# Attention of a hybrid encoder's first layer: scores, transposes and value products put into a woven order that is written out by hand for three engines

## The chip, the cores and the metric

The kernel runs as one program on one core of a Trainium2 chip. The metric is the time of one execution on the device in microseconds (us), taken over several runs. The core has five engines that work side by side, each through its own queue in order: TensorE (PE, matrix products and transposes; its weight loads are shown apart as PEld), VectorE (DVE), ScalarE (ACT), GpSimd (POOL), and SyncE (SP), which here only starts transfers. PE writes into PSUM, which the kernel uses as eight banks; here only DVE and ACT read them.

## The reference

Two residual layers, each a token mixer and a convolutional FFN, over 512 tokens of width 1024. The mixer of the first layer is windowed attention with 16 query heads, 4 key heads, width 64 of a head, and a sink logit for each head:

```
q, k, v = split(h @ w_qkv);  q = rope(rms_norm(q));  k = rope(rms_norm(k))
# for each block of 128 queries: the keys of the block before, its own and the next one
sc = q @ k.T * 64**-0.5;  sc = where(abs(qpos - kpos) <= 128, sc, -1e30)
m = max(max(sc), sink);  p = exp(sc - m)
o = (p @ v) / (sum(p) + exp(sink - m))
x = x + o @ w_o;  x = x + conv_ffn(rms_norm(x))
```

The second layer has RWKV-7 time mixing instead of attention. The change touches the attention alone.

## The kernel before

**Order of the work.** A planner (the kernel is built with `schedule_with_timeline_sim=True`, L1525) puts each engine's instructions into an order by its own model of their times; a tile takes the next free buffer of its pool, and waits are put in where data or a buffer needs them. Operations on `nc.any` get their engine from the planner. In the attention nothing else binds the order. (The scan of the second layer already holds each engine to the order of its program text, by a chain of order-only dependencies.)

**Up to the attention.** `swa` (L207) makes q, k and v in three groups `g` of 512 columns: group 0 holds all keys and 4 query heads, group 1 holds 8 query heads, group 2 the last 4 query heads and the values `vn`. For every group and each of 4 token tiles, `heads` (L249) calls `normed` (L223): a square on ACT (L227), a reduce and a scale on DVE (L229, L230), a power on POOL (L231), a product on DVE (L232), the gain on POOL (L233), six small rope operations on DVE (L242 to L247); then a rounded copy on ACT (L264), the remainder on POOL (L265 for groups 1 and 2), four transposes on PE (L271) and a copy out of PSUM on `nc.any` (L278). Groups 0 and 1 are done in place. The four calls for group 2 are kept back (`work`, L343) and stand in the program text ahead of head pairs 1 and 2 (`K.hw = (1, 2)`, L1279): token tiles 0 and 1 before pair 1, tiles 2 and 3 before pair 2. Only pairs 6 and 7 use the query heads of group 2.

**The attention.** The loop at L350 runs over 8 head pairs `hp`, inside it over 4 query blocks `n`, inside it over the 2 heads `e` of the pair. The first and the last block see 2 blocks of keys (256 columns of scores), the two in the middle see 3 (384 columns). For one (n, e): two score products in one PSUM bank (L367) and one product for each masked block (L370); the row maximum on DVE (L373), its negative against the sink (L374, one column), exp with the row sum on ACT (L376). Then for one n: 4 or 6 transposes of p into two banks `tp` (L382), their two copies to `pT` on `nc.any` (L384), and 4 or 6 value products (L387) that use half of the array's columns each (`128*64`; the profile shows two records for each of them) and add into the pair's bank `po`. After the 4 blocks: 1/denominator (L391 to L394), spread over 64 columns on ACT (L396), four transposes (L399), a copy on ACT (L401), the product with `po` on DVE (L402), and the split of the result into a rounded part on ACT (L97) and a remainder on DVE (L98). PSUM: 4 banks `sc`, 2 banks `tp`, 2 banks `mm` (`po` and the output transposes).

**After it.** `out_proj` (L144) multiplies by w_o: 8 output tiles of 24 products of 512 columns (L104 to L106), weights two blocks ahead (`ahead`, L75), in the banks `sc`. Seven eighths of a tile need the results of pairs 0 to 6 only.

Of the kernel before, what the change touches and what calls it, by code (L numbers as in the profile page):

```python
# [8 lines left out]
F32 = mybir.dt.float32  # L9
F32R = mybir.dt.float32r  # L10
BF16 = mybir.dt.bfloat16
AF = mybir.ActivationFunctionType
ALU = mybir.AluOpType
AX = mybir.AxisListType
PSUM = bass.MemoryType.PSUM

P = 128
S = 512
# [4 lines left out]
HD = 64  # L23
NB = 4
# [50 lines left out]
def ahead(K, blocks):  # L75

    raws = [load(K, *b[:2]) for b in blocks[:2]]
    nxt = weights(K, *blocks[0], raws[0])
    for i in range(len(blocks)):
        cur = nxt  # L80
        if i + 2 < len(blocks):
            raws.append(load(K, *blocks[i + 2][:2]))
        if i + 1 < len(blocks):
            nxt = weights(K, *blocks[i + 1], raws[i + 1])
        yield cur
# [10 lines left out]
def split(K, hi, lo, src, lo_engine):  # L96
    K.nc.scalar.copy(out=hi, in_=src)  # L97
    lo_engine.tensor_tensor(out=lo, in0=src, in1=hi.bitcast(F32), op=ALU.subtract)  # L98


def mm3(K, ps, lhs, rhs, first, last):

    nc = K.nc
    nc.tensor.matmul(ps, lhsT=lhs[0], rhs=rhs[0], start=first, stop=False)  # L104
    nc.tensor.matmul(ps, lhsT=lhs[0], rhs=rhs[1], start=False, stop=False)  # L105
    nc.tensor.matmul(ps, lhsT=lhs[1], rhs=rhs[0], start=False, stop=last)  # L106
# [37 lines left out]
def out_proj(K, w, oh, ol, on_tile, bank):  # L144

    for ot, (hi, lo) in enumerate(ahead(K, [(w[i], KT * P, K.nc.vector) for i in range(KT)])):
        ps = bank()
        for kt in range(KT):
            sl = slice(kt * P, (kt + 1) * P)
            mm3(K, ps, (hi[:, sl], lo[:, sl]), (oh[kt], ol[kt]), kt == 0, kt == KT - 1)  # L150
        on_tile(ot, ps)
# [55 lines left out]
def swa(K, x_in, xT, w_qkv, w_o, gains, sinks, rope, cst_mask, on_tile):  # L207
    nc = K.nc
    tc = K.tc
    with ExitStack() as es:  # L210
        ap = es.enter_context(tc.tile_pool(name="swa", bufs=1, reuse_waits="tile"))
        aw = es.enter_context(tc.tile_pool(name="swaw", bufs=2, reuse_waits="tile"))
        sm = es.enter_context(tc.tile_pool(name="swas", bufs=4, reuse_waits="tile"))
        pa = es.enter_context(tc.tile_pool(name="swap", bufs=4, space=PSUM, reuse_waits="tile"))
        pt = es.enter_context(tc.tile_pool(name="swapt", bufs=2, space=PSUM, reuse_waits="tile"))

        qT = K.act.tile([P, 2, KT, S], F32R, name="hl1").rearrange("p a k s -> p (a k) s")
        kT = ap.tile([P, NKV, 2, S], F32R, name="kT")
        vn = ap.tile([P, NB, NKV * HD], F32, name="vn")
# [60 lines left out]
        for g in (0, 1, 2):  # L280
# [33 lines left out]
            if g == 0:  # L314
                K.late()
                gk = ap.tile([P, 2 * HD], F32, name="gk")
                nc.sync.dma_start(out=gk, in_=gains)
                nsk = ap.tile([P, NH], F32, name="nsk")
                nc.sync.dma_start(out=nsk, in_=sinks)
                rp = ap.tile([P, NB, 16], F32, name="rp")  # L320
                nc.sync.dma_start(out=rp, in_=rope)
                mk = aw.tile([P, 2, 384], F32, name="p")[:, 0, 0:2 * P]
                nc.sync.dma_start(out=mk, in_=cst_mask)
                mkb = ap.tile([P, 2 * P], BF16, name="mkb")
                nc.vector.tensor_copy(out=mkb, in_=mk)
                idb = ap.tile([P, P], BF16, name="idb")
                nc.vector.tensor_copy(out=idb, in_=K.ident)
                gq = ap.tile([P, 12, HD], F32, name="gq")
                nc.gpsimd.tensor_copy(out=gq[:, 0:4], in_=gk[:, None, HD:].broadcast_to([P, 4, HD]))
                nc.gpsimd.tensor_scalar(out=gq[:, 4:], in0=gk[:, None, 0:HD].broadcast_to([P, 8, HD]), scalar1=HD ** -0.5,  # L330
                                        scalar2=None, op0=ALU.mult)
                nc.vector.tensor_scalar(out=nsk, in0=nsk, scalar1=-1.0, scalar2=None, op0=ALU.mult)
# [3 lines left out]
            for t in range(NB):  # L336
                nat = aw.tile([P, 512], F32, name="nat", bufs=4)
                nc.scalar.activation(out=nat[:, :w], in_=pss[t][:, :w], func=AF.Copy, scale=rst[:, t:t + 1])
                if g == 2:
                    nc.vector.tensor_scalar(out=vn[:, t], in0=pss[t][:, 256:], scalar1=rst[:, t:t + 1], scalar2=None,  # L340
                                            op0=ALU.mult)
                nats.append(nat)
            work = [(heads, (g, t, nats[t], nk, nh)) for t in range(NB)]  # L343
# [3 lines left out]

        ohl = K.act0.tile([P, 2, KT, S], F32R, name="hl0")
        oh, ol = ohl[:, 0], ohl[:, 1]
        for hp in range(8):  # L350
            if hp in K.hw:
                for fn, args in work[2 * K.hw.index(hp):2 * K.hw.index(hp) + 2]:
                    fn(*args)
            kv = hp // 2
            po = K.pmm.tile([P, NB, P], F32, name="mm")
            nm = sm.tile([P, NB, 2], F32, name="nm")
            den = sm.tile([P, NB, 2], F32, name="den")
            for n in range(NB):
                j0 = 1 if n == 0 else 0
                j1 = 2 if n == NB - 1 else 3  # L360
                bl = [j for j in (0, 2) if j0 <= j < j1]
                p = aw.tile([P, 2, 384], F32, name="p")
                for e in range(2):
                    sc = pa.tile([P, S], F32, name="sc")
                    sv = sc[:, j0 * P:j1 * P]
                    for z in range(2):
                        nc.tensor.matmul(sv, lhsT=qT[:, 2 * hp + e, n * P:(n + 1) * P],  # L367
                                         rhs=kT[:, kv, z, (n - 1 + j0) * P:(n - 1 + j1) * P], start=z == 0, stop=False)
                    for j in bl:
                        nc.tensor.matmul(sc[:, j * P:(j + 1) * P], lhsT=idb, rhs=mkb[:, j * HD:j * HD + P],  # L370
                                         start=False, stop=j == bl[-1])
                    m = sm.tile([P, 1], F32, name="m")
                    nc.vector.tensor_reduce(out=m, in_=sv, axis=AX.X, op=ALU.max)  # L373
                    nc.vector.scalar_tensor_tensor(out=nm[:, n, e:e + 1], in0=m, scalar=-1.0, in1=nsk[:, 2 * hp + e:2 * hp + e + 1],  # L374
                                                   op0=ALU.mult, op1=ALU.min)
                    nc.scalar.activation(out=p[:, e, j0 * P:j1 * P], in_=sv, func=AF.Exp, bias=nm[:, n, e:e + 1],  # L376
                                         accum_out=den[:, n, e:e + 1])
                pT = aw.tile([P, 2, 384], F32, name="pT")
                for e in range(2):
                    tp = pt.tile([P, S], F32, name="tp")  # L380
                    for j in range(j0, j1):
                        nc.tensor.transpose(out=tp[:, j * P:(j + 1) * P], in_=p[:, e, j * P:(j + 1) * P],  # L382
                                            identity=K.ident)
                    nc.any.tensor_copy(out=pT[:, e, j0 * P:j1 * P], in_=tp[:, j0 * P:j1 * P])  # L384
                for j in range(j0, j1):
                    for e in range(2):
                        nc.tensor.matmul(po[e * HD:(e + 1) * HD, n], lhsT=vn[:, n - 1 + j, kv * HD:(kv + 1) * HD],  # L387
                                         rhs=pT[:, e, j * P:(j + 1) * P], start=n == 0 and j == j0,
                                         stop=n == NB - 1 and j == j1 - 1)
            es_ = sm.tile([P, NB, 2], F32, name="es")  # L390
            nc.vector.tensor_tensor(out=es_, in0=nm, in1=nsk[:, None, 2 * hp:2 * hp + 2].broadcast_to([P, NB, 2]), op=ALU.subtract)  # L391
            nc.scalar.activation(out=es_, in_=es_, func=AF.Exp)
            nc.vector.tensor_tensor(out=den, in0=den, in1=es_, op=ALU.add)
            nc.vector.reciprocal(out=den, in_=den)  # L394
            o = aw.tile([P, NB, P], F32, name="o")
            nc.scalar.copy(out=o.rearrange("p n (e d) -> p n e d", e=2), in_=den[:, :, :, None].broadcast_to([P, NB, 2, HD]))  # L396
            oT = K.pmm.tile([P, NB, P], F32, name="mm")
            for n in range(NB):
                nc.tensor.transpose(out=oT[:, n], in_=o[:, n], identity=K.ident)  # L399
            o = aw.tile([P, NB, P], F32, name="o").rearrange("p n q -> p (n q)")  # L400
            K.e_o(out=o, in_=oT.rearrange("p n q -> p (n q)"))  # L401
            nc.vector.tensor_tensor(out=o, in0=po.rearrange("p n q -> p (n q)"), in1=o, op=ALU.mult)  # L402
            split(K, oh[:, hp], ol[:, hp], o, nc.vector)
        out_proj(K, w_o, [oh[:, i] for i in range(KT)], [ol[:, i] for i in range(KT)], on_tile,
                 lambda: pa.tile([P, S], F32, name="sc"))

# [1123 lines left out]
```

## Time and profile before

| what | value |
|---|---|
| three timed runs | 1616.32, 1618.85 (median), 1850.56 us |
| profiled execution, its own time | 1614.49 us |
| its span, first to last instruction | 1612.3 us |
| mean granted PE clock | 0.944 |
| busy PE / DVE / ACT / POOL | 92% / 64% / 43% / 27% of the span |
| attention, first scores to last value products | about 82.6 to 192.6 us of the span |

A row of a timeline gives start, duration, engine, line, operation, output<-input and count, with the idle time before it in square brackets where there was any. Durations on one engine overlap: the next instruction of a stream starts before the one ahead of it has ended, so the distance between two starts, not the duration, is what an instruction takes from its engine. A PE that is busy all the time is therefore not PE at its peak.

### The profile page before, as it was taken

What the parts mean: (1) busy time and instruction counts of PE and PEld (TensorE: products, weight loads), DVE (VectorE), ACT (ScalarE), POOL (GpSimd) and SP (SyncE); (2) the same over time, 40 slices, a digit from 0 to 9 for tenths busy, and PEclk for the clock granted to TensorE, in tenths of its full rate; (3) what the DMA queues carried; (4) which work ended last, traced back from release to release, by engine and by line L of the source; (5) the groups of instructions that cost most, each with busy time, mean ns of one, the idle gap of its engine ahead of it and who ended that gap; (6) DMA issues with size and microseconds to landing.
All of it is one profiled execution on the core that took longest, in us unless ns stands there. A gap on an engine that the chain in (4) does not pass through costs nothing. (4 is left out here: it accounts for less than half of the span.)

```text
span 1612.3 us, 28487 instructions
## 1 busy us (share of the span) xinstructions
PE 1479.9 (92%) x11612; PEld 1195.5 (74%) x11612; DVE 1035.2 (64%) x1642; ACT 687.3 (43%) x1227; POOL 442.2 (27%) x533
## 2 busy tenths in 40 slices
PE   8999999999999998989986678888589999999999
PEld 7767688888888886767764577777467788888887
DVE  6876447777763348968988557667256677777222
ACT  5576534444442223655543333434334444444111
POOL 2630002322310015425498422332200323222000
PEclk9999999999999999999986588888899999999999
DMA  5200033223333322446546545555532222333341
GB/s 191 75 27 1 18 92 97 96 92 105 92 98 117 108 83 68 138 157 217 177 143 199 160 107 145 147 142 147 165 106 84 91 92 91 97 99 101 101 121 56
DMA packets 108978, 179.09 MB, mean 111 GB/s; under 512 B 49200, under 2 KB 62128, under 8 KB 108848
## 3 DMA queue, kind: packets, MB, share of 16 engines
q1 hardware_dynamic: 108704, 177.27, 35.6%
q8 instruction: 91, 1.49, 0.4%
q14 instruction: 39, 0.32, 0.1%
q10 hardware_dynamic: 144, 0.00, 0.0%
HBM read 142.91 MB, written 34.34 MB: 110 GB/s over the span
## 5 line engine op out<-in xcount | busy, mean ns | idle before, releaser
L68 ACT CAST whi<-wraw 128x1024 fp32r<-128x1024 f32 (+2 forms) x196 | 200.3, 1023 | 275.5 <-PE mm L105 179.4
L71 DVE TENSOR_TENSOR wlo<-wraw,whi 128x1024 fp32r<-128x1024 f32 (+2 forms) x139 | 167.6, 1207 | 183.4 <-ACT whi L68 182.7
L104 PE MATMUL mm<-hl,whi 128*128 128x512 f32 x720 | 281.3, 391 | 1.5 <-DVE xT L1360 0.9
L106 PE MATMUL mm<-hl,wlo 128*128 128x512 f32 x720 | 281.5, 391 | 0.5 <-POOL wlo L71 0.4
L105 PE MATMUL mm<-hl,whi 128*128 128x512 f32 x720 | 281.1, 391 | 0.4 <-DVE hl L92 0.4
L71 POOL TENSOR_TENSOR wlo<-wraw,whi 128x1024 fp32r<-128x1024 f32 x57 | 137.1, 2405 | 413.0 <-ACT whi L68 413.0
L185 DVE SCALAR_TENSOR_TENSOR conv<-upad,par,conv 128x512 f32<-128x512 f32 x88 | 125.6, 1429 | 64.0 <-ACT conv L182 64.0
L106 PEld LDWEIGHTS mm<-hl,wlo 128*128 128x128 f32 x720 | 135.5, 188 | 31.6 <-POOL wlo L71 2.3
L104 PEld LDWEIGHTS mm<-hl,whi 128*128 128x128 f32 x720 | 135.6, 188 | 29.8 <-ACT hl L91 1.3
L105 PEld LDWEIGHTS mm<-hl,whi 128*128 128x128 f32 x720 | 135.6, 188 | 29.4 <-DVE hl L92 1.1
L106 PE MATMUL mm<-gh,wlo 128*128 128x512 f32 x352 | 139.0, 395 | 0.0
L104 PE MATMUL mm<-gh,whi 128*128 128x512 f32 x352 | 139.0, 395 | 0.0
L105 PE MATMUL mm<-gl,whi 128*128 128x512 f32 x352 | 139.0, 395 | 0.0
L97 ACT CAST gh<-gact 128x512 fp32r<-128x512 f32 x44 | 27.3, 621 | 141.4 <-DVE gact L194 141.4
L182 ACT ACTIVATE conv<-upad,par 128x512 f32<-128x512 f32 x88 | 71.6, 815 | 21.5 <-DVE upad L180 21.4
L106 PEld LDWEIGHTS mm<-gh,wlo 128*128 128x128 f32 x352 | 66.1, 188 | 16.1
L105 PEld LDWEIGHTS mm<-gl,whi 128*128 128x128 f32 x352 | 66.1, 188 | 16.0
L104 PEld LDWEIGHTS mm<-gh,whi 128*128 128x128 f32 x352 | 66.1, 188 | 16.0
L997 POOL TENSOR_TENSOR tg<-X,Y 128x56 f32<-128x56 f32 (+16 forms) x129 | 46.7, 362 | 111.0 <-DVE Y L999 81.6
L187 DVE SCALAR_TENSOR_TENSOR conv<-upad,par,conv 128x512 f32<-128x512 f32 x88 | 70.1, 798 | 3.0
L192 ACT ACTIVATE silu<-conv 128x512 f32<-128x512 f32 x44 | 27.8, 632 | 91.3 <-DVE conv L187 91.3
L106 PE MATMUL mm<-sx,wlo 128*128 128x512 f32 (+1 forms) x144 | 59.1, 410 | 2.9 <-DVE wlo L71 2.9
(334 smaller groups left out, 3109.6 us busy)
## 6 DMA issues: line engine op xcount, KB each, us to landing
wraw<-in_w_up_dram SPq DMA_DIRECT2D x88, 512.0 KB, 3.6
wraw<-in_w_down_dram SPq DMA_DIRECT2D x32, 512.0 KB, 3.5
ars<-tab SPq DMA_DIRECT2D x16, 512.0 KB, 2.9
bks<-tab SPq DMA_DIRECT2D x16, 512.0 KB, 3.3
ar<-ars SPq DMA_DIRECT2D x8, 1024.0 KB, 8.7
bk<-bks SPq DMA_DIRECT2D x8, 1024.0 KB, 6.5
wraw<-in_w_down_dram SPq DMA_DIRECT2D x16, 384.0 KB, 3.2
wraw<-in_w_qkv_dram SPq DMA_DIRECT2D x11, 512.0 KB, 4.1
```

The lines of the kernel that those rows point to most:

```text
L68: nc.scalar.copy(out=hi, in_=raw)
L71: lo_engine.tensor_tensor(out=lo, in0=raw, in1=hi.bitcast(F32), op=ALU.subtract)
L97: K.nc.scalar.copy(out=hi, in_=src)
L104: nc.tensor.matmul(ps, lhsT=lhs[0], rhs=rhs[0], start=first, stop=False)
L105: nc.tensor.matmul(ps, lhsT=lhs[0], rhs=rhs[1], start=False, stop=False)
L106: nc.tensor.matmul(ps, lhsT=lhs[1], rhs=rhs[0], start=False, stop=last)
L182: nc.scalar.activation(out=c, in_=u[:, 1:S + 1], func=AF.Identity, scale=K.par[:, cw + 2 * FT + ch:cw + 2 * FT + ch + 1], bias=K.par[:, cb ...
L185: nc.vector.scalar_tensor_tensor(out=c, in0=u[:, 0:S], scalar=K.par[:, cw + ch:cw + ch + 1], in1=c, op0=ALU.mult, op1=ALU.add)
L187: nc.vector.scalar_tensor_tensor(out=c, in0=u[:, 2:S + 2], scalar=K.par[:, cw + 4 * FT + ch:cw + 4 * FT + ch + 1], in1=c, op0=ALU.mult, op ...
L192: nc.scalar.activation(out=sg, in_=acts[0], func=AF.Silu)
L997: en.tensor_tensor(out=tm, in0=X[:, 0:kx, kx:kx + 1].broadcast_to([P, kx, n]), in1=Y[:, kx:kx + 1, m:16].broadcast_to([P, kx, n]), op=ALU. ...
```

## The change

- The loop over pairs and blocks becomes a loop of 18 units `u`, two blocks each. In unit u the scores of two blocks of pair u//2 alternate with the transposes of the two blocks that came two ahead: scores, transposes, scores, transposes. The value products of the two transposed blocks come at the end of the unit, together.
- The exps of a block are put after the copies of the transposed block.
- Both heads' maxima go into one tile and one operation of two columns makes both biases.
- The copies out of the transposes have fixed engines: DVE for the first head of the pair, ACT for the second.
- p has its own buffers (`pe`, 4 in place of 2); the first load of the mask uses one of them.
- The spreading of 1/denominator goes from ACT to POOL. It stands one unit ahead of the rest of the pair's ending (`heads_out`), which comes at the end of an odd unit, before that unit's value products on PE. The output transposes use a bank `tp` in place of `mm`.
- Everything that the 18 units put on PE, DVE and ACT, the kept-back calls of `heads` included, is chained in the order of the text, each engine for itself. POOL, SP and operations on `nc.any` are outside the chain.

The removed loop is the one printed above; it is left out here.

```diff
--- before.py
+++ after.py
@@ -319,7 +319,7 @@
                 nc.sync.dma_start(out=nsk, in_=sinks)
                 rp = ap.tile([P, NB, 16], F32, name="rp")
                 nc.sync.dma_start(out=rp, in_=rope)
-                mk = aw.tile([P, 2, 384], F32, name="p")[:, 0, 0:2 * P]
+                mk = aw.tile([P, 2, 384], F32, name="pe", bufs=4)[:, 0, 0:2 * P]
                 nc.sync.dma_start(out=mk, in_=cst_mask)
                 mkb = ap.tile([P, 2 * P], BF16, name="mkb")
                 nc.vector.tensor_copy(out=mkb, in_=mk)
@@ -347,60 +347,119 @@
 
         ohl = K.act0.tile([P, 2, KT, S], F32R, name="hl0")
         oh, ol = ohl[:, 0], ohl[:, 1]
...
+        def span(n):
+            return (1 if n == 0 else 0), (2 if n == NB - 1 else 3)
+
+        def scores(hp, c, n):
+
             kv = hp // 2
...
+            j0, j1 = span(n)
+            bl = [j for j in (0, 2) if j0 <= j < j1]
+            c.p[n] = aw.tile([P, 2, 384], F32, name="pe", bufs=4)
+            m = sm.tile([P, 2], F32, name="m")
+            svs = []
+            for e in range(2):
+                sc = pa.tile([P, S], F32, name="sc")
+                sv = sc[:, j0 * P:j1 * P]
+                for z in range(2):
+                    nc.tensor.matmul(sv, lhsT=qT[:, 2 * hp + e, n * P:(n + 1) * P],
+                                     rhs=kT[:, kv, z, (n - 1 + j0) * P:(n - 1 + j1) * P], start=z == 0, stop=False)
+                for j in bl:
+                    nc.tensor.matmul(sc[:, j * P:(j + 1) * P], lhsT=idb, rhs=mkb[:, j * HD:j * HD + P],
+                                     start=False, stop=j == bl[-1])
+                nc.vector.tensor_reduce(out=m[:, e:e + 1], in_=sv, axis=AX.X, op=ALU.max)
+                svs.append(sv)
+            nc.vector.scalar_tensor_tensor(out=c.nm[:, n], in0=m, scalar=-1.0, in1=nsk[:, 2 * hp:2 * hp + 2],
+                                           op0=ALU.mult, op1=ALU.min)
+            def exps():
+                for e in range(2):
+                    nc.scalar.activation(out=c.p[n][:, e, j0 * P:j1 * P], in_=svs[e], func=AF.Exp, bias=c.nm[:, n, e:e + 1],
+                                         accum_out=c.den[:, n, e:e + 1])
+            return exps
+
+        def turned(c, n):
+            j0, j1 = span(n)
+            c.pT[n] = aw.tile([P, 2, 384], F32, name="pT")
+            for e in range(2):
+                tp = pt.tile([P, S], F32, name="tp")
+                for j in range(j0, j1):
+                    nc.tensor.transpose(out=tp[:, j * P:(j + 1) * P], in_=c.p[n][:, e, j * P:(j + 1) * P],
+                                        identity=K.ident)
+                if e:
+                    nc.scalar.copy(out=c.pT[n][:, e, j0 * P:j1 * P], in_=tp[:, j0 * P:j1 * P])
+                else:
+                    nc.vector.tensor_copy(out=c.pT[n][:, e, j0 * P:j1 * P], in_=tp[:, j0 * P:j1 * P])
+
+        def summed(hp, c, n):
+            kv = hp // 2
+            j0, j1 = span(n)
+            for j in range(j0, j1):
+                for e in range(2):
+                    nc.tensor.matmul(c.po[e * HD:(e + 1) * HD, n], lhsT=vn[:, n - 1 + j, kv * HD:(kv + 1) * HD],
+                                     rhs=c.pT[n][:, e, j * P:(j + 1) * P], start=n == 0 and j == j0,
+                                     stop=n == NB - 1 and j == j1 - 1)
+
+        def weights_of(hp, c, k):
+
+            if k == 0:
+                c.es = sm.tile([P, NB, 2], F32, name="es")
+                nc.vector.tensor_tensor(out=c.es, in0=c.nm, in1=nsk[:, None, 2 * hp:2 * hp + 2].broadcast_to([P, NB, 2]),
+                                        op=ALU.subtract)
+                nc.scalar.activation(out=c.es, in_=c.es, func=AF.Exp)
+                return
+            nc.vector.tensor_tensor(out=c.den, in0=c.den, in1=c.es, op=ALU.add)
+            nc.vector.reciprocal(out=c.den, in_=c.den)
+            c.o = aw.tile([P, NB, P], F32, name="o")
+            nc.gpsimd.tensor_copy(out=c.o.rearrange("p n (e d) -> p n e d", e=2), in_=c.den[:, :, :, None].broadcast_to([P, NB, 2, HD]))
+
+        def heads_out(hp, c):
+            oT = pt.tile([P, S], F32, name="tp")
             for n in range(NB):
...
+                nc.tensor.transpose(out=oT[:, n * P:(n + 1) * P], in_=c.o[:, n], identity=K.ident)
             o = aw.tile([P, NB, P], F32, name="o").rearrange("p n q -> p (n q)")
...
+            K.e_o(out=o, in_=oT)
+            nc.vector.tensor_tensor(out=o, in0=c.po.rearrange("p n q -> p (n q)"), in1=o, op=ALU.mult)
             split(K, oh[:, hp], ol[:, hp], o, nc.vector)
+
+        ins = nc.cur_bb.bb.instructions
+        mark = ins[-1]
+        pairs = []
+        for u in range(18):
+            if u < 16 and u % 2 == 0:
+                hp = u // 2
+                if hp in K.hw:
+                    for fn, args in work[2 * K.hw.index(hp):2 * K.hw.index(hp) + 2]:
+                        fn(*args)
+                c = Ctx()
+                c.p, c.pT = {}, {}
+                c.nm = sm.tile([P, NB, 2], F32, name="nm")
+                c.den = sm.tile([P, NB, 2], F32, name="den")
+                c.po = K.pmm.tile([P, NB, P], F32, name="mm")
+                pairs.append(c)
+            hp, b = (u - 1) // 2, 2 * ((u - 1) % 2)
+            for k in range(2):
+                if u and u <= 16 and b and k == 0:
+                    weights_of(hp, pairs[hp], 0)
+                exps = scores(u // 2, pairs[u // 2], 2 * (u % 2) + k) if u < 16 else None
+                if u and u <= 16 and b and k == 0:
+                    weights_of(hp, pairs[hp], 1)
+                if u and u <= 16:
+                    turned(pairs[hp], b + k)
+                if exps:
+                    exps()
+            if u > 2 and u % 2:
+                heads_out((u - 3) // 2, pairs[(u - 3) // 2])
+            if u and u <= 16:
+                for n in (b, b + 1):
+                    summed(hp, pairs[hp], n)
+        start = next(k for k in reversed(range(len(ins))) if ins[k] is mark) + 1
+        held = {e.engine: None for e in (nc.tensor, nc.vector, nc.scalar)}
+        for x in ins[start:]:
+            if x.engine in held:
+                if held[x.engine] is not None:
+                    tc.add_manual_dep(x, held[x.engine].name, mybir.DependencyInfo(
+                        mybir.DependencyClass.NoSync, mybir.DependencyReason.DATA), reason="order")
+                held[x.engine] = x
         out_proj(K, w_o, [oh[:, i] for i in range(KT)], [ol[:, i] for i in range(KT)], on_tile,
                  lambda: pa.tile([P, S], F32, name="sc"))
```

## Rows read from the trace of the kernel before

**Rows 1.** Busy time of engines in one stretch (us, busy, records), clock, DMA share, GB/s.
```profile
150.00:160.00 10.00, 10.00 (x80) 7.24 (x78) 7.01 (x23) 7.26 (x24) 0.00 (x0) 1.00 0.00 0
```

**Rows 2.** One line's instructions: the first operation of a pair's ending.
```profile
L391 DVE TENSOR_TENSOR es<-nm,nsk x8: 154/160/168, 97.6 to 176.6; 128x8 f32<-128x8 f32 x8
```

**Rows 3.** Timeline of PE inside one pair.
```profile
147.91 0.60 PE L399 MATMUL mm<-ident,o 128*128 128x128 f32 x4
148.27 0.60 PE L367 MATMUL sc<-kT,hl 128*128 128x384 f32 x2
...
148.92 0.87 PE L387 MATMUL mm<-pT,vn 128*64 128x128 f32 x10
149.72 0.44 PE L382 MATMUL tp<-ident,p 128*128 128x128 f32 x2
...
150.57 0.43 PE L387 MATMUL mm<-pT,vn 128*64 128x128 f32 x2
150.94 0.44 PE L382 MATMUL tp<-ident,p 128*128 128x128 f32 x2
```

**Rows 4.** Timeline of DVE inside one pair.
```profile
149.03 0.56 DVE L373 TENSOR_REDUCE m<-sc 128x1 f32<-128x384 f32 x1 [1.09 <-PE sc L370]
...
150.68 0.56 DVE L373 TENSOR_REDUCE m<-sc 128x1 f32<-128x384 f32 x1
151.27 0.16 DVE L374 SCALAR_TENSOR_TENSOR nm<-m,nsk 128x1 f32<-128x1 f32 x1
...
152.67 0.41 DVE L384 COPY pT<-tp 128x256 f32<-128x256 f32 x1
153.00 0.75 DVE L373 TENSOR_REDUCE m<-sc 128x1 f32<-128x256 f32 x2
```

**Rows 5.** Timeline of ACT inside one pair.
```profile
147.38 0.47 ACT L376 ACTIVATE p<-sc,nm 128x256 f32<-128x256 f32 x1 [0.37 <-PE tp L382]
...
148.29 0.37 ACT L384 COPY pT<-tp 128x256 f32<-128x256 f32 x1
```

**Rows 6.** Timeline of DVE at the end of the last pair.
```profile
192.74 0.69 DVE L402 TENSOR_TENSOR o<-mm,o 128x512 f32<-128x512 f32 x1 [9.82 <-PE mm L387]
194.11 0.69 DVE L98 TENSOR_TENSOR hl<-o,hl 128x512 fp32r<-128x512 f32 x1 [0.68 <-ACT hl L97]
```

**Rows 7.** Timeline of ACT at the end of the last pair.
```profile
193.46 0.62 ACT L97 CAST hl<-o 128x512 fp32r<-128x512 f32 x1 [1.54 <-DVE o L402]
```

**Rows 8.** Timeline of PE there.
```profile
194.13 0.73 PE L104 MATMUL sc<-hl,whi 128*128 128x512 f32 x2 [1.50 <-ACT hl L97]
```

**Rows 9.** Groups of 78 to 118 us, shapes apart: busy, mean ns, idle before.
```profile
L233 POOL TENSOR_TENSOR nat<-nat,gq 128x256 f32<-128x256 f32 x4 | 4.1, 1036 | 1.0 <-DVE nat L232 1.0
L231 POOL TENSOR_TENSOR hss<-hss,mhalf 128x4 f32<-128x4 f32 x4 | 4.1, 1036 | 2.6 <-DVE hss L230 2.4
...
L265 POOL TENSOR_TENSOR hl<-nat,hl 128x256 fp32r<-128x256 f32 x4 | 2.9, 729 | 10.3 <-PE sc L370 6.9 <-ACT hl L264 3.4
L232 DVE TENSOR_TENSOR nat<-nat,hss 128x256 f32<-128x256 f32 x4 | 2.4, 599 | 0.0
...
L227 ACT ACTIVATE hsq<-nat 128x256 f32<-128x256 f32 x4 | 1.7, 414 | 0.9 <-DVE hss L229 0.9
L229 DVE TENSOR_REDUCE hss<-hsq 128x4 f32<-128x256 f32 x4 | 1.6, 408 | 0.1
```

**Rows 10.** One line's instruction: the copy on POOL that spreads a gain.
```profile
L329 POOL COPY gq<-gk x1: 983/983/983, 15.8 to 15.8; 128x256 f32<-128x256 f32 x1
```

**Rows 11.** Timeline of POOL between 82.5 and 88.6 us.
```profile
84.23 2.66 POOL L233 TENSOR_TENSOR nat<-nat,gq 128x256 f32<-128x256 f32 x2
```

**Rows 12.** Timeline of DVE in the same stretch.
```profile
86.23 0.68 DVE L374 SCALAR_TENSOR_TENSOR nm<-m,nsk 128x1 f32<-128x1 f32 x1
```

**Rows 13.** PE alone by stretches: us, busy (records), clock, DMA share, GB/s.
```profile
86.00:87.00 1.00, 0.56 (x4) 1.00 0.00 0
...
88.00:89.00 1.00, 1.00 (x6) 0.50 0.91 360
```

More of the change, by code (lines that the diff above doesn't have):

```diff
@@ L349, in swa @@
         oh, ol = ohl[:, 0], ohl[:, 1]
[L350 to L353, printed above, removed]
+        def span(n):
+            return (1 if n == 0 else 0), (2 if n == NB - 1 else 3)
+        def scores(hp, c, n):
             kv = hp // 2
-            po = K.pmm.tile([P, NB, P], F32, name="mm")
-            nm = sm.tile([P, NB, 2], F32, name="nm")
-            den = sm.tile([P, NB, 2], F32, name="den")
-            for n in range(NB):
[L359 to L399, printed above, removed]
@@ L400, in swa @@
+        def heads_out(hp, c):
+            oT = pt.tile([P, S], F32, name="tp")
+            for n in range(NB):
+                nc.tensor.transpose(out=oT[:, n * P:(n + 1) * P], in_=c.o[:, n], identity=K.ident)
             o = aw.tile([P, NB, P], F32, name="o").rearrange("p n q -> p (n q)")
-            K.e_o(out=o, in_=oT.rearrange("p n q -> p (n q)"))
-            nc.vector.tensor_tensor(out=o, in0=po.rearrange("p n q -> p (n q)"), in1=o, op=ALU.mult)
+            K.e_o(out=o, in_=oT)
+            nc.vector.tensor_tensor(out=o, in0=c.po.rearrange("p n q -> p (n q)"), in1=o, op=ALU.mult)
```

## The prediction, made before the changed kernel ran

> **What bounds the kernel now.** I read the busy shares by stretches first: inside the attention PE is busy all of the time while DVE and ACT have a third free [rows 1]. The reader should then see how regular it is: the first operation of a pair's ending starts at 97.6 us for pair 0 and at 176.6 for pair 7, so a pair takes (176.6 - 97.6) / 7 = 11.28 us [rows 2]. The timeline of PE says what fills them [rows 3]. Four transposes take 0.36 from start to start. Ten records of value products take 0.80 and two take 0.37, so one costs (0.80 - 0.37) / 8 = 0.054 and a run of them 0.26 on top. A pair of 384-column scores takes 0.65 ahead of a value run, and I put 0.12 of that down to the same switch between whole-array products and half-array ones. The trace has 8 value runs in a pair (of 2, 6 or 10 records), 40 records in all: 8 x 0.38 + 40 x 0.054 = 5.2. Twenty transposes at 0.1 are 2.0, the output transposes 0.4; the remaining 3.7 are scores. The sum is the whole period: the stage is bound by what PE takes from start to start, a quarter of it switches.
>
> **The change on PE.** Two runs of 20 records in a pair: 2 x 0.38 + 40 x 0.054 = 2.9 in place of 5.2. PE alone would need 11.28 - 2.3 = 9.0 a pair. That is the gain on offer: 7 x 2.3 = 16 us.
>
> **The chain that takes its place.** The order is now that of the text on PE, DVE and ACT, so I follow one pair through it, from the start of the scores of block 2. Prices from start to start: scores of 384 columns reach DVE 0.76 after their start [rows 3, 4]; a reduce to its dependent operation 0.59 for 384 columns, 0.45 for 256; a copy of 256 columns 0.33 (of 384 some 0.48), a reduce that isn't waited for the same; a two-column bias 0.16, the next start 0.07 after it [rows 4]; two exps of 256 columns 1.0 with the last readout [rows 5].
> - Block 2 to the exps of block 3: 0.76, second head 0.54 later, 0.59 + 0.07, copy 0.33, reduces 0.33 + 0.44, bias 0.2: 3.25. ACT then has a copy to end (0.35) and two exps (1.0): 4.6.
> - The ending of the pair before (`heads_out`) now lies here, ACT, DVE, ACT, DVE by turns, each waiting for the other: copy 0.6, product 0.69, rounding 0.62, remainder 0.6, handovers 0.03 each [rows 6, 7]: 2.6, so 7.2. In the kernel before, the planner put it between other work; now DVE can't reduce the scores of the next pair, long done, before the remainder.
> - Next pair's block 0: difference 0.08, reduces and bias 0.85, sum and reciprocal 0.3, copy 0.48; block 1: reduces and bias 1.1, copy 0.4: 3.25, so 10.45.
> - The second half of the value run waits for that last copy: 8 records and the switch, 0.7. Only then come PE's scores of block 2: 11.2.
>
> So PE waits about 2 us in each pair; all three engines stand in one ring.
>
> **The copy moved to POOL.** It saves ACT 0.6, off the ring. The trace has no copy of 512 columns with spreading on POOL; one of 256 took 0.98 [rows 10], so between 1.0 and 2.0; I take 1.9, twice the columns. It has a unit's time for itself, but not for its neighbours: while POOL multiplied two SBUF operands (84.23 to 86.89), the bias operation on DVE, 0.16 alone, took 0.68 and ended with it [rows 4, 11, 12]. The copy starts at about 8.5 and the bias of block 1 at 9.9, so it would be held to 10.4: +0.45, and the ring is 11.6. Weighed: the Trainium skill, "SBUF — State Buffer", section "SBUF: two separate sides", says that GpSimd holds a port pair for its whole instruction and that DVE operations with two SBUF inputs wait. By it the ring is 11.6; by the chain alone it is 11.2, 3 us less over seven pairs.
>
> **The stops.** The kept-back `heads` calls are inside the chain too, one token after the other: ACT may not begin the second token before the first one's rounded copy. One token: square 0.41, reduce 0.41, scale 0.16, power 1.04, product 0.4 to 0.6, gain 0.73 to 1.04 (mean, and POOL's product of that size for the remainder), rope 0.8 (six operations of at most 0.16), rounded copy 0.4 [rows 4, 9]: 4.4 to 4.9, and 0.3 for eight handovers; 4.9 taken. Two tokens and the last remainder and transposes (0.73 + 0.45): 11.0 us in which PE, DVE and ACT have nothing else, since scores, reduces and exps stand behind. POOL is outside the chain but has nothing to do before ACT and DVE feed it; the copies on `nc.any` are outside as well and wait for PE. Work moved here: 4 squares, 4 rounded copies, 36 DVE operations, 16 transposes; no transfer. After a stop the ring starts anew with two blocks, 4.65 + 0.45 to the scores of block 2. For pair 1 the stop begins at the last exps, 1.4 after the point of [rows 2]: 1.4 + 11.0 + 5.1 + 3.2 = 20.7. For pair 2 it begins after `heads_out`: 3.35 + 11.0 + 5.1 + 3.2 = 22.65. Over two plain pairs: +9.1 and +11.05, 20.1 together.
>
> **Around it.** Before pair 0's ending the four tokens' work is gone: between 0 and 5.4 us earlier (the ring alone from the first scores of block 2); 4 taken, as PE's projection ahead stays. At the other end PE fills with the output projection; five of its seven last value runs go (5 x 0.38 = 1.9) and so should the 1.50 of idle before the last eighth [rows 8]: -3.5. Cover: the last ending needs about 8 us after the last exps (it stands behind that of pair 6 and has the POOL copy in it), and PE then has 12 of work left.
>
> Merged biases save 4 x 0.07 of DVE a pair, already in the ring; four buffers of p and of `tp` cost nothing, they are freed two blocks ahead.
>
> **Sum.** Ring 7 x 11.6 - 79.0 = +2.2; stops +20.1; start -4; end -3.5: +14.8 on the profiled execution's 1614.49 = 1629.3. The lowest and the median of the timed runs lie 1.8 and 4.4 above it; I add 2: **1631 us**.
>
> **Clock.** PE was at 0.56 busy and then ran at 0.50 of its clock, 1.2 GHz, for a stretch [rows 13]. Both stops leave it idler than that. The Trainium skill, "TensorE: Matmul & The Clock Gate", Part 1, says that an idle PE is throttled and activity releases it; by that, each restart would cost some 2 us more, 1635. I leave it to the range.
>
> **Rivals.**
> - PE stays the bound: the ring has slack that I don't see, a pair takes 9.0 to 9.5. For: DVE and ACT are busy for seven tenths only [rows 1]. Against: those are sums, the ring is an order. Five plain pairs by 2.6 less: 14.8 - 13 = +2, **1618**. Chance 0.17.
> - The stops don't come about: the order holds less than it says, or the tokens' work still hides beside the pairs, as it does now. Against: squares, reduces and transposes are on held engines. 14.8 - 20.1 = -5, **1611**; with the rival above too, -23, **1593**. Chance 0.12.
> - Slower by a mechanism of its own: with PE waiting 2 to 3 us in every pair, the clock falls through the stage. The ring holds some 2.5 us of PE (scores to DVE, value run); at half clock they double. 7 x 2.5 + 4 for the stops: +36, **1652**. For: [rows 13]. Against: PE still works four fifths of the time; it decides only if nearly all pairs are hit. Chance 0.11.
>
> The forecast has 0.60 (1620 to 1642 of its own, by the ends of POOL's copy, the tokens and the start). Range 1607 to 1648: it takes in the first rival, the better part of the third's near end, and leaves out most of the second. About 2%, 32 us, is what a measurement can tell from no change: faster (under 1586) needs both gains and more, 0.03; slower (over 1651) is half of the last rival and a tail of the forecast, 0.08; within, 0.89.
>
> **What would show it.** Value runs of 20 records, two a pair: step one. A DVE that sits idle for ACT's exps and roundings in the middle of odd units, and pair endings 11 to 12 us apart: the ring; 9 apart: the first rival. Two holes of about 11 us in PE ahead of pairs 1 and 2 with POOL as the last releaser: the stops; no holes: the second. A granted clock near 0.5 in 120 to 190 us: the third. A bias operation of 0.5 us or more under POOL's copy: the port. I am wrong if the attention's last value product comes before 192 us of the span.

## The result: 1.0% slower, 1634.7 us

The changed kernel took **1634.68 us** (median of 6 runs, 1629.30 to 1637.79) against 1616.44 us of the kernel before (6 runs; the one of 1850.56 is left out of the ratio). The ratio is **1.0102, 95% interval 1.0084 to 1.0120**: by it 16.5 us more, within the 2% that one measurement tells from no change, and not zero. The forecast was 1631. The profiled execution has a span of 1632.9 us (before 1612.3) and a mean granted clock of 0.930 (before 0.944).

**Where the time is measured.** The difference of the spans, 20.6, is not all of the change. This is one line's group in the changed kernel (duration min/median/max in ns, first and last start): the down projections of both FFNs. Line numbers are those of the changed kernel from here on.

```profile
L104 PE MATMUL mm<-gh,whi x352: 392/394/399, 486.7 to 1628.2; 128*128 128x512 f32 x176
```

Their first start, after the attention, was at 470.9 before and is at 486.7: +15.8. From there to the last start the program text is the same in both, and took 1136.7 before and 1141.5 here; in the twelve variants below it took 1135.0 to 1147.7. That scatter is larger than most of what follows. So single executions are compared at a **marker**, the start of the last eighth of the output projection ([rows 8]: 194.13), and times by their ratios.

```profile
198.33 0.60 PE L418 MATMUL tp<-ident,o 128*128 128x128 f32 x4
...
206.97 0.66 PE L418 MATMUL tp<-ident,o 128*128 128x128 f32 x4
209.72 0.73 PE L104 MATMUL sc<-hl,whi 128*128 128x512 f32 x2 [2.10 <-ACT hl L97]
```

That is PE's timeline at the end of the attention: the output transposes of pairs 6 and 7, and the marker, at 209.72, which is **+15.6**. The idle time ahead of it is 2.10, where [rows 8] had 1.50.

**The pairs.** The changed kernel's DVE timeline, the bias of block 3 of pairs 0, 1, 2, 3 and 7 (in the kernel before, the row of [rows 2] follows this bias at once):

```profile
92.01 0.16 DVE L372 SCALAR_TENSOR_TENSOR nm<-m,nsk 128x2 f32<-128x2 f32 x1
...
114.26 0.16 DVE L372 SCALAR_TENSOR_TENSOR nm<-m,nsk 128x2 f32<-128x2 f32 x1
...
138.34 0.16 DVE L372 SCALAR_TENSOR_TENSOR nm<-m,nsk 128x2 f32<-128x2 f32 x1
...
149.32 0.16 DVE L372 SCALAR_TENSOR_TENSOR nm<-m,nsk 128x2 f32<-128x2 f32 x1
...
193.23 0.16 DVE L372 SCALAR_TENSOR_TENSOR nm<-m,nsk 128x2 f32<-128x2 f32 x1
```

Two distances hold a stop (22.25 and 24.08); the other five are 43.91 + 10.98 = 54.89, so a plain pair takes **10.98**, against 11.28 in [rows 2]. All seven take 101.22; before it was 79.0.

**A plain pair.** PE's timeline from the end of one pair to the next scores of block 2:

```profile
161.04 0.63 PE L418 MATMUL tp<-ident,o 128*128 128x128 f32 x4 [0.73 <-ACT pT L389]
161.60 1.31 PE L398 MATMUL mm<-pT,vn 128*64 128x128 f32 x20
162.84 0.51 PE L365 MATMUL sc<-kT,hl 128*128 128x256 f32 x2
...
167.57 0.66 PE L398 MATMUL mm<-pT,vn 128*64 128x128 f32 x8 [0.21 <-DVE pT L391]
168.16 0.61 PE L365 MATMUL sc<-kT,hl 128*128 128x384 f32 x2
```

The value runs are those forecast (20 records in 1.24 from start to start, in place of the short ones in [rows 3]), and PE now waits, 0.73 and 0.21 here and 0.44 between them, 1.4 of a pair's 10.98, where [rows 1] had it full. DVE in the same stretch:

```profile
160.38 0.56 DVE L391 COPY pT<-tp 128x384 f32<-128x384 f32 x1
162.32 0.69 DVE L421 TENSOR_TENSOR o<-mm,o 128x512 f32<-128x512 f32 x1 [1.39 <-ACT o L420]
163.69 0.69 DVE L98 TENSOR_TENSOR hl<-o,hl 128x512 fp32r<-128x512 f32 x1 [0.68 <-ACT hl L97]
164.31 0.16 DVE L406 TENSOR_TENSOR es<-nm,nsk 128x8 f32<-128x8 f32 x1
164.38 0.75 DVE L370 TENSOR_REDUCE m<-sc 128x1 f32<-128x256 f32 x2
...
167.03 0.16 DVE L372 SCALAR_TENSOR_TENSOR nm<-m,nsk 128x2 f32<-128x2 f32 x1
167.10 0.42 DVE L391 COPY pT<-tp 128x256 f32<-128x256 f32 x1
```

The scores that DVE reduces at 164.38 began on PE at 162.84 and were ready well before. DVE stands for ACT's copy (1.39) and for ACT's rounding (0.68), and the last copy, at 167.10, releases PE's eight records at 167.57. That is the ring. POOL's copy in it:

```profile
165.80 0.61 POOL L413 COPY o<-den 128x512 f32<-128x512 f32 x1 [10.36 <-PE tp L386]
```

**The stops.** PE at the first one, and ACT:

```profile
92.11 1.58 PE L398 MATMUL mm<-pT,vn 128*64 128x128 f32 x20
99.26 1.12 PE L271 MATMUL tp<-ident,hl 128*128 128x128 f32 x4 [5.58 <-POOL hl L265]
104.00 1.11 PE L271 MATMUL tp<-ident,hl 128*128 128x128 f32 x4 [3.62 <-POOL hl L265]
104.76 0.78 PE L365 MATMUL sc<-kT,hl 128*128 128x256 f32 x2
...
111.15 0.62 PE L365 MATMUL sc<-kT,hl 128*128 128x384 f32 x2
```

```profile
93.54 0.44 ACT L227 ACTIVATE hsq<-nat 128x256 f32<-128x256 f32 x1
98.00 0.40 ACT L264 CAST hl<-nat 128x256 fp32r<-128x256 f32 x1 [4.01 <-DVE nat L247]
98.31 0.41 ACT L227 ACTIVATE hsq<-nat 128x256 f32<-128x256 f32 x1
```

The second token's square starts only behind the first one's rounded copy, 4.77 after the first. PE does eight transposes in 11 us, and its restart to the scores of block 2 takes 6.39. The table by stretches (us, busy and records of PE, PEld, DVE, ACT, POOL, then the clock) says at which clock:

```profile
90.00:100.00 10.00, 4.37 (x40) 3.46 (x40) 4.39 (x17) 4.18 (x14) 3.00 (x4) 0.78 0.00 1
100.00:110.00 10.00, 6.38 (x34) 5.03 (x34) 4.11 (x16) 3.21 (x10) 2.52 (x4) 0.54 0.01 2
...
120.00:130.00 10.00, 2.87 (x12) 2.38 (x13) 3.14 (x18) 2.41 (x6) 3.90 (x5) 0.50 0.00 0
130.00:140.00 10.00, 9.26 (x75) 7.37 (x76) 6.16 (x18) 5.92 (x21) 0.61 (x1) 0.85 0.02 3
140.00:150.00 10.00, 8.67 (x86) 6.63 (x82) 7.30 (x21) 6.13 (x20) 0.61 (x1) 1.00 0.00 0
```

Around both stops the clock is at its half level, 1.2 GHz, and between them it comes back (0.97 from 110 to 120); from 140 to 200 it is full, though PE waits in every pair.

### The profile page after: what moved, and what is told of

It reads as the page before. It is cut to its first block, busy times and chain, and to the rows that moved or that the text cites. A ratio compares the mean times of both kernels' runs of the same rounds, so it can differ in the third digit from the quotient of the medians.

```text
span 1632.9 us, 28471 instructions
## 1 busy us (share of the span) xinstructions
PE 1480.7 (91%) x11612; PEld 1204.0 (74%) x11612; DVE 1031.1 (63%) x1613; ACT 681.8 (42%) x1216; POOL 446.4 (27%) x541
```

## The experiments

All edits are to the changed kernel. A time is the median of 4 to 10 executions and a ratio is to the kernel before, run beside it, unless one execution is named; marker, pairs and stretches are read from one profiled execution each.

**1. The head calls out of the chain.** Only their PE, DVE and ACT instructions are freed; the rest stays in order.

```
-        pairs = []
+        pairs, free = [], set()
...
+                    n0 = len(ins)
                     for fn, args in work[2 * K.hw.index(hp):2 * K.hw.index(hp) + 2]:
                         fn(*args)
+                    free.update(x.name for x in ins[n0:])
...
-            if x.engine in held:
+            if x.engine in held and x.name not in free:
```

> The changed kernel, but the kept-back token work (heads of group 2) stays at its place in the text and is left out of the chain. Theory (two stops, and a ring in every pair): both stops of some 11 us and the slow restart behind each go, some 4 us of the work come back ahead of pair 0's ending: the last eighth of the output projection starts at 186 to 191 us of the span in place of 209.7, the time is 1610 to 1617, and pairs still come every 11.0 us. Rival (the tokens' 36 DVE operations and POOL steps cost as much anywhere, since DVE is in the ring): the work lands in the ring, pairs 0 to 2 grow, the marker is at 200 to 205 and the time 1625 to 1630.

Measured: 1614.86 us, ratio 0.9978 (0.9957 to 0.9999). Marker and the table by stretches, where the first stop had been:

```profile
189.19 1.20 PE L104 MATMUL sc<-hl,whi 128*128 128x512 f32 x2 [2.10 <-ACT hl L97]
```

```profile
100.00:110.00 10.00, 9.05 (x92) 7.07 (x90) 6.36 (x18) 7.17 (x23) 0.69 (x2) 1.00 0.01 2
```

The stops are gone, the clock is full, the plain pairs are unchanged (10.98) and the marker comes 20.5 sooner. So the head calls in the order are the whole of the loss, and more: without them the change is a shade faster than before, by 0.2%, which its interval only just tells from nothing.

**2. No chain at all**: the new text, each engine ordered by the planner.

```
-        for x in ins[start:]:
+        for x in ():
```

> The changed kernel with no chain at all: same program text, order by the planner. Theory: the order is what costs, not the regrouping; no stops, endings put between other work, pairs every 9.0 to 11.3 us, time 1598 to 1616. Rival (the regrouping, the copy on POOL and the fixed copy engines cost by themselves): no holes in PE, but pairs stay near 11 and more, time 1618 to 1635.

Measured: 1614.84 us, ratio 0.9978 (0.9962 to 0.9994), marker 193.68, pairs 11.06. PE's value runs in a part of one pair:

```profile
152.50 0.65 PE L398 MATMUL mm<-pT,vn 128*64 128x128 f32 x6
...
154.79 0.43 PE L398 MATMUL mm<-pT,vn 128*64 128x128 f32 x2
```

The planner cuts them as in [rows 3], and PE is busy all of the time again (9.96 to 10.0 of 10). The long runs come from the order, not from the text.

**3. PE kept busy in the stops.** Sixteen products of 512 columns, whose results nobody reads, ahead of the transposes of each kept-back call.

```
                 tp = pt.tile([P, S], F32, name="tp")
+                if g == 2:
+                    for _ in range(16):
+                        nc.tensor.matmul(tp, lhsT=qT[:, 0, 0:P], rhs=kT[:, 0, 0], start=True, stop=True)
```

> The changed kernel with 16 extra products of 512 columns ahead of each kept-back token's transposes, whose result is thrown away: PE works through the two stops instead of idling. Theory (the stops cost their length by the tokens' chain, and the half clock behind them costs apart): the stops stay 11.1 and 11.4 us long, the granted clock stays at 1.00 between 94 and 134 us, and the restart from the next scores of block 0 to those of block 2 takes 4.6 to 4.9 us in place of 6.4: marker 205.5 to 207.5, time 1630 to 1632. Rival (the clock costs nothing here, DVE and ACT set the restart): marker 209 to 210.

Measured: 1624.65 us, ratio 1.0046 (1.0029 to 1.0062), marker 205.53. PE's timeline (L368 here is L365 above) and two stretches:

```profile
93.84 4.00 PE L271 MATMUL tp<-kT,hl 128*128 128x512 f32 x16
...
104.69 0.48 PE L368 MATMUL sc<-kT,hl 128*128 128x256 f32 x2
...
109.10 0.62 PE L368 MATMUL sc<-kT,hl 128*128 128x384 f32 x2
```

```profile
100.00:110.00 10.00, 9.61 (x72) 7.35 (x70) 4.48 (x19) 4.70 (x14) 2.80 (x4) 1.00 0.01 2
...
120.00:130.00 10.00, 8.15 (x56) 6.51 (x58) 4.66 (x22) 4.10 (x12) 3.82 (x5) 1.00 0.01 2
```

The first stop ends where it did (104.69 against 104.76), but the restart takes 4.41, not 6.39, a little less than the 4.6 to 4.9 expected. The half clock therefore cost 4.2 at the marker. Work for nothing made the kernel faster. The time is lower than the 1630 to 1632 expected; in the profiled executions that lies in the untouched part, 1135.0 here and 1141.5 in the changed kernel.

**4. Two links of the ring.** First, DVE's remainder of the pair's result one unit later, behind copies that DVE has to make anyway:

```
-            split(K, oh[:, hp], ol[:, hp], o, nc.vector)
+            nc.scalar.copy(out=oh[:, hp], in_=o)
+            c.lo = lambda: nc.vector.tensor_tensor(out=ol[:, hp], in0=o, in1=oh[:, hp].bitcast(F32), op=ALU.subtract)
...
+                if k and u > 3 and u % 2 == 0:
+                    pairs[(u - 4) // 2].lo()
                 if exps:
...
+                if u == 17:
+                    pairs[7].lo()
```

> The changed kernel with one operation moved: the DVE remainder of a pair's result goes from the end of the odd unit to behind the next unit's second copy out of the transposes. Theory (the ending lies in the ring): DVE no longer waits for ACT's rounding ahead of the next reduces; pairs every 9.9 to 10.2 us in place of 10.97, five of them and the stop's second half gain some 5 us, the marker is at 204 to 206. Rival (PE or the sum of DVE's work sets the pair): 10.97 stays, marker 209 to 210.

Measured: 1624.91 us, ratio 1.0053 (1.0034 to 1.0072), marker 204.67, pairs 10.09: 0.9 less each. On DVE the subtraction of L406, which stood behind the wait for ACT's rounding (164.31 above), now follows the product at once:

```profile
150.79 0.69 DVE L421 TENSOR_TENSOR o<-mm,o 128x512 f32<-128x512 f32 x1 [1.39 <-ACT o L420]
151.40 0.16 DVE L406 TENSOR_TENSOR es<-nm,nsk 128x8 f32<-128x8 f32 x1
```

Second, the value run of a unit behind the first scores of the next one:

```
+                if u > 1 and k == 0:
+                    for n in range(2 * (u % 2), 2 * (u % 2) + 2):
+                        summed((u - 2) // 2, pairs[(u - 2) // 2], n)
...
-            if u and u <= 16:
-                for n in (b, b + 1):
-                    summed(hp, pairs[hp], n)
```

> The changed kernel with the value products of a unit moved behind the first scores of the next unit on PE. Theory: the other closure of the ring (value run waits for DVE's last copy, the next scores wait for the run) opens, but the ending still stands in DVE's way: pairs every 10.4 to 10.7 us, marker 206 to 208. Rival (the wait of the value run is the whole of PE's idle time): 9.5 or less. Rival (neither matters): 10.97.

Measured: 1630.44 us, ratio 1.0086 (1.0061 to 1.0111), marker 208.24, 0.2 above the forecast; pairs 10.49, 0.49 less. Both links lie in the ring.

**5. POOL's copy back on ACT**, where the kernel before had it.

```
-            nc.gpsimd.tensor_copy(out=c.o.rearrange("p n (e d) -> p n e d", e=2), in_=c.den[:, :, :, None].broadcast_to([P, NB, 2, HD]))
+            nc.scalar.copy(out=c.o.rearrange("p n (e d) -> p n e d", e=2), in_=c.den[:, :, :, None].broadcast_to([P, NB, 2, HD]))
```

> The changed kernel with the spreading of 1/denominator back on ACT. Theory (that copy lies beside the ring): pairs 10.9 to 11.3 us, marker 209 to 212. Rival (ACT is short of time in the ring, and moving the copy to POOL was worth its 0.6 us): pairs 11.5 or more, marker 213 or later. Rival (a POOL copy holds DVE up): pairs 10.7 or less.

Measured, in one execution (1630.53 us): pairs 11.37, marker 211.20. ACT's timeline:

```profile
154.65 0.62 ACT L413 COPY o<-den 128x512 f32<-128x512 f32 x1 [1.02 <-DVE den L411]
155.17 0.47 ACT L389 COPY pT<-tp 128x384 f32<-128x384 f32 x1
```

On ACT it stands ahead of the copy of a transposed block and costs 0.39 a pair, between the theory's end (11.3) and the rival's (11.5): that part of the change gains, a little more than expected.

**6. These edits together.** The head calls out of the chain (1) and the remainder later (the first of 4):

> The changed kernel with the token work out of the chain and the remainder moved, the value run left at the unit's end. Theory: no stops, pairs of 10.1 us, marker 183 to 185, time 1607 to 1612.

With the value run later as well (the second of 4):

> The changed kernel with the token work out of the chain, the remainder moved back and the value run moved behind the next unit's first scores, all three. Theory (two closures of one ring: the ending on DVE, and value run and scores on PE): with both open a pair takes 9.4 to 9.8 us, near the 9.0 that PE needs; the marker (last eighth of the output projection) is at 179 to 183 us, the time 1604 to 1609. Rival (the single gains of 0.9 and 0.5 don't add, one wait takes the other's place): pairs 10.0 to 10.1, marker 183 to 185, time 1609 to 1612.

Measured: 1606.70 us, ratio 0.9933 (0.9916 to 0.9951), pairs 10.08, marker 183.48; and 1606.89 us, ratio 0.9929 (0.9913 to 0.9944), pairs 9.59, marker 180.97. Both beat both kernels. Their markers are 2.5 apart, their times are not told apart. With all three PE is at 9.38 of 10 us busy in a pair of 9.59, which is 9.0 of work: the figure that the prediction gave PE alone. A stretch of that kernel:

```profile
140.00:150.00 10.00, 9.38 (x97) 7.77 (x95) 7.81 (x25) 6.95 (x24) 0.62 (x1) 1.00 0.01 2
```

**7. The end.** Here the prediction's term was off, and the first attempt at it failed.

```
+            if u == 16:
+                last = next(x for x in reversed(ins) if x.engine == nc.tensor.engine).name
...
+        mark = ins[-1]
...
                  lambda: pa.tile([P, S], F32, name="sc"))
+        start = next(k for k in reversed(range(len(ins))) if ins[k] is mark) + 1
+        for x in ins[start:]:
+            if x.engine == nc.tensor.engine:
+                tc.add_manual_dep(x, last, mybir.DependencyInfo(
+                    mybir.DependencyClass.NoSync, mybir.DependencyReason.DATA), reason="order")
```

> The changed kernel, in which every PE instruction of the output projection stands behind the last PE instruction of the attention itself (the last value product and the last scores). In the changed kernel's trace 21 projection products stand ahead of the output transposes of pair 6, ACT waits 4.21 us for those transposes, and the last eighth of the projection begins 2.10 us late, at 209.72 us. Theory: the ending of the last pair is what the end of the attention waits for, and the projection's early products hold it up. Then the output transposes come some 3 to 4 us sooner, the wait of the last eighth goes, PE has no hole there, and the last eighth begins at 207.5 to 208.5. Rival: PE needs those early products to fill the time of the last ending, and with them behind it idles instead: the last eighth begins at 209.7 or later. Pairs 10.97 apart by both, stops unchanged.

The instruction named `last` is the value run of unit 15; the last transposes, the last value run and the output transposes of pair 7 come after it, so the hold is narrower than the expectation's first sentence says. Measured, in one execution (1635.84 us): marker 211.04, **later**, against the theory. PE's timeline:

```profile
203.90 0.88 PE L398 MATMUL mm<-pT,vn 128*64 128x128 f32 x12
...
207.69 0.66 PE L398 MATMUL mm<-pT,vn 128*64 128x128 f32 x8
208.28 0.66 PE L418 MATMUL tp<-ident,o 128*128 128x128 f32 x4
211.04 0.81 PE L104 MATMUL sc<-hl,whi 128*128 128x512 f32 x2 [2.10 <-ACT hl L97]
```

Pair 6's transposes did come 4.4 sooner (193.96), but the planner then put twelve projection products into the last value run. The rival's number came, not its reason: PE idles 2.10 as before, and not more. (Ahead of pair 6's transposes the changed kernel has 23 products, where the expectation counts 21.) The same in the kernel with the earliest marker so far:

> The kernel with the head calls out of the order, the remainder and the value run one unit later (marker 180.97, 1606.9 us), with every PE instruction of the output projection behind the attention's last one. Theory: as in the run beside it, the wait of 1.16 us ahead of the last eighth goes and the last eighth begins at 179 to 180.5; the time 1604 to 1607 us. Rival: the early products were filling time that PE then idles, and the marker stays at 181 or comes later, the time 1607 to 1610.

Measured: 1607.17 us, ratio 0.9924 (0.9903 to 0.9944), marker 184.14: 3.2 later, its last value runs cut too. The way from the last output transposes to the marker stays the same: 2.75 in the changed kernel and here, 2.76 in experiment 6 with all three and in the run above. So PE has to keep products for that time. Twelve held back, of the first two tiles with the heads of pairs 5 and 6:

```
...
                  lambda: pa.tile([P, S], F32, name="sc"))
...
+        mm = [x for x in ins[start:] if x.engine == nc.tensor.engine]
+        for x in mm[15:21] + mm[39:45]:
+            tc.add_manual_dep(x, held[nc.tensor.engine].name, mybir.DependencyInfo(
+                mybir.DependencyClass.NoSync, mybir.DependencyReason.DATA), reason="order")
```

> The changed kernel, in which twelve products of the output projection (those of its first two tiles with the heads of pairs 5 and 6) stand behind PE's last instruction of the attention, the output transposes of pair 7; all other products are where the planner puts them. Theory, formed on the three ends seen so far: from the start of those transposes to the first product of the last eighth it is 2.75 us in each (206.97 to 209.72 in the changed kernel, 178.21 to 180.97 and 208.28 to 211.04 in two others), whatever stands before; PE idles in it by what it has already spent of its free products. Then twelve products of 0.23 fill it, the output transposes come about 2.8 us sooner, and the last eighth begins at 206.9 to 207.4 with no idle time ahead of it. Rival: the transposes of the weights of the last unit wait for ACT and DVE rather than for PE's products, so that PE only idles earlier, and the last eighth stays at 209 or later.

Measured, in one execution (1640.22 us): the marker has no idle time ahead of it, but comes at 209.32:

```profile
204.22 0.66 PE L386 MATMUL tp<-ident,pe 128*128 128x128 f32 x4 [0.62 <-ACT pT L389]
...
206.05 0.66 PE L418 MATMUL tp<-ident,o 128*128 128x128 f32 x4
206.46 0.49 PE L104 MATMUL sc<-hl,whi 128*128 128x512 f32 x1
...
209.32 0.61 PE L104 MATMUL sc<-hl,whi 128*128 128x512 f32 x2
```

Half of each theory: the hole of 2.10 is filled, a hole of 0.62 for ACT opens ahead of the last transposes of p, and this execution was 1.0 late already at the last pair's L406 (202.6 against 201.6). From there to the marker it is 6.76 instead of 8.16: 1.4 gained, not 2.8. Twelve is also more than the way needs: it is 3.27 here, not 2.75. With all three edits:

> The kernel with the head calls out of the order, the remainder and the value run one unit later (marker 180.97 with 1.16 us of idle ahead of it, 1606.9 us), with the same twelve products behind the attention's last PE instruction. Theory: the idle 1.16 us goes and the last eighth begins at 179.7 to 180.0; a timed ratio 0.0007 lower than without it, less than the comparison can tell, 1604 to 1608 us. Rival: 181 unchanged, PE idle earlier instead.

Measured: **1602.03 us, ratio 0.9904 (0.9886 to 0.9922)**, marker 180.86, without idle time ahead of it. This execution too was 0.6 late at the last L406 (172.7 against 172.1); from there to the marker it gained 0.7, where 1.0 to 1.3 was expected, and PE now idles earlier:

```profile
175.97 0.44 PE L386 MATMUL tp<-ident,pe 128*128 128x128 f32 x2 [0.41 <-ACT pT L389]
```

The time is below the 1604 to 1608 expected, and the ratio is the lowest of all; but the marker is only 0.1 sooner, and by the intervals the ratio can't be told from 0.9929. That the twelve products made it faster is not shown.

## Why the prediction was right, step by step

The mechanism was right: PE freed, a ring in its place, two stops. Experiment 1 shows the stops, 3 and 4 the clock and the ring. The sum was +14.8 and the marker says +15.6, but that closeness is partly luck; four terms were mis-sized.

- **PE alone 9.0, value runs of 20: right.** The runs are seen in PE's timeline, the 9.0 in experiment 6. "PE waits about 2 us in each pair" was 1.4: in the changed kernel one of the two runs is cut into 12 and 8 records by a wait, and PE is busy for 9.6 of 10.98.
- **Ring 11.2 by the chain, 11.6 with POOL's hold: 10.98.** The way through the ring was right (experiment 4 took 0.9 and 0.5 out of it at two of its links). The term that failed is "I take 1.9" for POOL's copy, with bounds from 1.0 to 2.0: it took **0.61**. It ends at 166.41, and the bias at 167.03 comes after it, so nothing was held; five plain pairs came out 54.9, not 58.0. Its source misled: the 0.98 of [rows 10] was not what a copy of 256 columns takes by itself. In the kernel before it ran beside a DVE subtraction with two SBUF inputs, here the rows of both:

```profile
15.29 1.22 DVE L71 TENSOR_TENSOR wlo<-wraw,whi 128x1024 fp32r<-128x1024 f32 x1
...
15.78 0.98 POOL L329 COPY gq<-gk 128x256 f32<-128x256 f32 x1 [15.34 <-DMA gk<-in_gains_dram]
```

In all fourteen traces of this case that copy starts 0.34 to 0.49 after the subtraction's start, takes 0.98 to 1.14, and ends 0.25 to 0.26 after the subtraction's end. Its end goes with DVE's, so most of its time was waiting; no run has it without the subtraction. The rule of the Trainium skill, "SBUF — State Buffer", section "SBUF: two separate sides", on which the 0.45 leaned beside [rows 11, 12], agrees with that, with POOL as the side that waits. For the copy of 1/denominator it was neither borne out nor refuted: in no run does such a DVE operation start under it. "It saves ACT 0.6, off the ring" was wrong too: experiment 5 puts 0.39 a pair on it.

- **Stops 20.7 and 22.65: 22.25 and 24.08.** The work in them was sized right (a token 4.77 against 4.9; at full clock, in experiment 3, the two distances are 19.98 and 21.95). What was left to the range belonged into the sum: the half clock, 2.27 and 2.13 of it. Here the trace bears out the Trainium skill, "TensorE: Matmul & The Clock Gate", Part 1, that an idle PE is throttled and activity releases it; the estimate of 2 for each restart that stood beside it was close.
- **Start -4: -5.5**, just past the bound of 5.4 (92.1 against 97.6 for the same point). **End -3.5: -1.1.** The step "so should the 1.50 of idle before the last eighth" failed: cover of 12 us was there, but the planner spent it before it was needed, 23 products ahead of pair 6's output transposes. Experiment 7 shows that it is a matter of what PE still has behind the last output transposes: four products in the last kernel of experiment 6 left 1.16 of idle, none left 2.10, twelve left nothing there, but opened a hole ahead of the last transposes of p.
- Together: ring and stops 101.2 where 101.35 was forecast (-3.1 of ring, +3.0 of stops), start -1.5, end +2.4: +0.8. The rest of the distance from 1631 to 1634.7 lies outside the steps: the untouched part was 4.8 longer in the profiled execution. Why it scatters so, no run settles.
- **The rivals.** PE as the bound shows only when head calls, remainder and value run are all moved. The stops came. Half clock through the stage did not: 1.00 from 140 us on, with PE waiting 1.3 of 10 us.

## What to carry to other kernels

An order written out by hand turns every handover inside it into a link: before holding three engines to a text, follow one round through it, and put two-engine errands (round, then subtract) behind work that the engine has anyway. Leave filler work, such as the head calls here, out of the order, and what must fill the end inside it. A stop was dearer than its length, since PE came back at half clock (2.27 and 2.13 us here). And before a row becomes a price, read what the other engines did beside it: the 0.98 of POOL's copy was mostly a wait.

## What the runs showed of the hardware

POOL's spreading copy of 512 columns took 0.61 us, on ACT 0.62. A POOL copy of 256 columns [rows 10] that started inside a DVE subtraction with two SBUF inputs took 0.98 to 1.14, and in fourteen traces ended 0.25 to 0.26 us after that subtraction, wherever in it it had started. And sixteen products for nothing in each kept-back call, 4.0 us of PE, held the granted clock at 1.00 through two stops of 11 us, where it had fallen to 0.50. The marker shows 4.2 us of gain. The ratio fell by more (1.0102 to 1.0046, each against its own executions of the kernel before); in the profiled executions the rest lies in the untouched part, and no run says why.
